# Shift of the modulation as two extra token columns, with its weights read during the projection stream

## The chip, the cores and the metric

One core of one Trainium2 chip runs the kernel. The metric is the device time of one execution in microseconds, as the median of several runs. A run's profile gives the span of the core and what each engine did: PE (TensorE, with PEld for its weight loads), DVE (VectorE), ACT (ScalarE), POOL (GpSimd) and SP (SyncE, which here only issues transfers).

## The reference

One layer of a hybrid backbone over 640 tokens: 128 context tokens and 512 latent tokens. What matters here is the modulated norm and the one input projection behind it (D_MODEL = 2048, D_IN = 7216):

```python
mod_ctx = silu(c_ctx)[None] @ w_mod + b_mod      # the same with c for the latent tokens
shift, scale, gate = jnp.split(mod, 3, axis=-1)
h = _rms_norm(x, norm_w) * (1.0 + scale[:, None]) + shift[:, None]
proj = h @ w_in
u_f, z_f, qkv, z_d, ab = jnp.split(proj, [...], axis=-1)
y_f = _fourier_mix(u_f, grid) * jax.nn.silu(z_f)
qkv = _short_conv(qkv, conv_w)
...
y_d = _rms_norm(o, gnorm_w).reshape(bsz, l, D_DELTA) * jax.nn.silu(z_d)
y = jnp.concatenate([y_f, y_d], axis=-1) @ w_out
return x + gate[:, None] * y, ...
```

All arrays are float32. There are two modulation vectors, one for all context tokens and one for all latent tokens. q, k and v (12 heads of 128) go through a short convolution and a gated-delta scan in chunks, in both directions; the context's final states are an output, and a final norm follows the layer.

## The kernel before

The kernel works on transposed activations: 16 tiles h_hi and 16 tiles h_lo of 128 rows (model channels) by 640 tokens, float32 split into a high and a low part of a faster format. A projection tile is 128 output channels. It takes, for both token halves of 320 columns (HALVES) and all 16 row tiles, three matmuls (high weight by high h, high by low, low by high), 96 in all, written by `stream` (L1272). The weights come by ACT's DMA queue in loads of half a tile into two buffers raw (`loads`, L1242), ACT makes the high part (`casts`, L1251) and POOL the low part (`lows`, L1259), five buffers each.

The **prologue** reads x, transposes and norms it (xT), and computes the modulation in pairs of row tiles (eight pairs kp). For a pair of scales, `mod_load` issues four loads of 512 KB from w_mod on SP's queue, `mod_rows` multiplies them with the two condition vectors (L421), `mod_cols` transposes and adds the parts up (L429), and `spread` writes h_hi and h_lo of the pair. While the scales arrive, the tiles k, v and q of head 0 and the gate columns ab are accumulated from h without the shift (`early_part`, L408 and L409); they are stored to ed. The shift of a pair is computed by the same steps (`shift_rows`, `shift_cols`): its columns csh are written, and `spread` computes h_hi and h_lo of the pair a second time with the shift. Pairs 0 to 2 of the shift stand between scale pairs 3 to 7, pair 3 behind them, pairs 4 to 7 among the three Fourier tiles u0 to u2, which are computed in the prologue too (`u_part`, L540). `shift_product` (L545) multiplies the shift columns with the weights of head 0 and of the gates; the result, ebias, is added to the stored early tiles later (`early_bias`, L593).

Behind the prologue the order is written out by a planner. Steps of work are generators with a rank; a step yields the engine it needs next ("P", "A", "V", "G", "S") or "poll", and is taken up when the estimate of engine times (class Estimate) says that it is due on PE's time line. The estimate starts with all engines free at the stream's first instruction. On the chip, each engine runs its instructions in the order so written and waits for semaphores. The tiles follow one another in the order of `names`: k1 q1 v1 z0 u3, then k, v, q of a head and z of the head before, and at the end k11 v11 q11 z10 f0 f1 f2 f3 z11. At a tile's end the stream waits for what it needs: k and q of head i for the scan ("delta") of head i - 2, v for the reading of the v before.

What follows a tile: `conv` evicts q, k, v from PSUM into one of two padded tiles pj (L713) and convolves; `after_z` reads PSUM for the gates z and f (L746 tanh, L749 product) and stores them; `after_u` stores u. Per head there follow `blocks`, `solve` (small triangular blocks, through two transfers over DRAM), `decay` (its last step squares q on ACT into jq and sums by a matmul, L935 and L939), `prep`, `scan` and `head_out` (L1098). `gates` (L623 to L660) comes ahead of all heads. `res_gates` (L1202, L1212) computes the residual gate in eight blocks of 256 columns behind head 0's scan. `fourier` runs for four groups in two lanes and needs u, f, the last head's solve and the residual gates. Then the output pass (L1541) multiplies y with w_out, heads 0 to 10 first, then the four Fourier groups, then head 11.

Of the kernel before, what the change touches and what calls it, by code (L numbers as in the profile page):

```python
# [9 lines left out]
F32 = mybir.dt.float32  # L10
# [7 lines left out]
P = 128  # L18
# [194 lines left out]
def hybrid_step(ctx: ExitStack, tc: tile.TileContext, x_prompt, x_sample, state_ctx, c, c_ctx,  # L213
# [53 lines left out]

    wpool = ctx.enter_context(tc.tile_pool(name="wpool", bufs=1))
# [30 lines left out]
    with tc.tile_pool(name="start", bufs=1) as st:  # L299
# [42 lines left out]

        pm0 = mbank()
# [33 lines left out]
        hi_t = [big.tile([P, NT], F32R, tag=slots[k], name="h_hi") for k in range(NK)]  # L377
        lo_t = [big.tile([P, NT], F32R, tag=slots[NK + k], name="h_lo") for k in range(NK)]


        first = (C_K, C_V, C_Q)
# [7 lines left out]
        ahead = {3: 0, 5: 1, 7: 2}  # L389
        csh = st.tile([P, NK, 32], F32, name="csh")  # L390
# [43 lines left out]
        def spread(kt, shift):  # L434
            hf = st.tile([P, NT], F32, tag="hf", name="hf", bufs=1)
            for m, a, b in ((1, 0, P), (0, P, NT)):
                x, scm = xT[:, kt, a:b], sc[:, kt, m:m + 1]
                if shift:
                    sh = csh[:, kt, m:m + 1]
                    ACT.activation(hi_t[kt][:, a:b], x, AF.Identity, bias=sh, scale=scm)  # L440
                    DVE.tensor_scalar(hf[:, a:b], x, scm, sh, ALU.mult, ALU.add)
                else:
                    ACT.mul(hi_t[kt][:, a:b], x, scm)
                    DVE.tensor_scalar(hf[:, a:b], x, scm, None, ALU.mult)
            DVE.tensor_tensor(lo_t[kt], hf, hi_t[kt], ALU.subtract)

        def scales(kp, ms):
            mo = mod_cols(pms[0], ms)
            for i in range(2):
                kt = 2 * kp + i  # L450
                DVE.tensor_scalar(sc[:, kt], mo[:, i], cols[:, 16 + kt:17 + kt],
                                  cols[:, 48 + kt:49 + kt], ALU.add, ALU.mult)
            for i in range(2):
                spread(2 * kp + i, False)

        shift_ms = {}

        def shift_rows(kp):
            shift_ms[kp] = mod_rows(pms[1], mod_load(256 * kp))

        def shift_cols(kp):
            mo = mod_cols(pms[1], shift_ms.pop(kp))
            for i in range(2):
                kt = 2 * kp + i
                DVE.tensor_scalar(csh[:, kt, 0:2], mo[:, i], cols[:, kt:kt + 1], None, ALU.add)
            for i in range(2):
                spread(2 * kp + i, True)

        def load_rest(c):
            raws = [wpool.tile([P, 8, P], F32, tag="raw", name="raw", bufs=2) for _ in range(2)]  # L470
            ACT.dma_start(out=raws[0].rearrange("p (k u) b -> p k (u b)", u=2), in_=win_v[:, 4 * c:4 * c + 4, 0:256])
            ACT.dma_start(out=raws[1][:, 0:4], in_=win_v[:, 4 * c:4 * c + 4, 256:384])
            rv = raws[0].rearrange("p (k u) b -> p u k b", u=2)
            return rv[:, 0], rv[:, 1], raws[1][:, 0:4]

        def load_first(c):
            cr = []
            for j in range(2):
                x = st.tile([P, 4, 256], F32, tag="wm", name="cr", bufs=8).rearrange("p a b -> p (a b)")[:, 0:864]
                cr.append(x.rearrange("p (k n) -> p k n", k=2))  # L480
                ks = slice(4 * c + 2 * j, 4 * c + 2 * j + 2)
                for i in range(3):
                    SP.dma_start(out=cr[j][:, :, P * i:P * (i + 1)], in_=win_v[:, ks, first[i]:first[i] + P])
                POOL.tensor_copy(cr[j][:, :, 384:432], abr[:, ks])
            return cr
# [5 lines left out]
        for kp in range(NK // 2):  # L491
# [17 lines left out]
            if kp in ahead:  # L509
                shift_rows(ahead[kp])  # L510
# [6 lines left out]
            if kp in ahead:  # L517
                shift_cols(ahead[kp])
        shift_rows(3)
        early_part(NK // 2 - 1, 0, prev)  # L520
        shift_cols(3)
        rest = load_rest(0)
        ws = [split(rest[0]), split(rest[1])]
        cr = load_first(0)
# [6 lines left out]
        ws.append(split(rest[2]))  # L531
        u_res = [[bank(), bank()], [bank(), bank()], [bank(), mbank()]]
        pc = mbank()

        def u_part(i, c, w):
            for j in range(4):
                k = 4 * c + j
                for n, (x, h) in enumerate(((w[0], hi_t), (w[0], lo_t), (w[1], hi_t))):
                    for (a, b), acc in zip(HALVES, u_res[i]):
                        PE.matmul(acc[:, 0:320], lhsT=x[:, j, :], rhs=h[k][:, a:b], start=k + n == 0,  # L540
                                  stop=k == NK - 1 and n == 2)

        def shift_product(c, cr):
            for j in range(4):
                PE.matmul(pc[32 * j:32 * j + 32, 0:432], lhsT=csh[:, 4 * c + j, :], rhs=cr[j // 2][:, j % 2, :], start=c == 0,  # L545
                          stop=c == 3, tile_position=(0, 32 * j))

        for c in range(4):
            now, ws = ws, []
            if c < 3:  # L550
                rest = load_rest(c + 1)
            steps = [[4], [5, 6], [7], []][c]
            for i in range(3):
                if i < len(steps):
                    shift_rows(steps[i])
                u_part(i, c, now[i])
                if i < len(steps):
                    shift_cols(steps[i])
                if c < 3 and i > 0:
                    ws += [split(x) for x in (rest[0:2] if i == 1 else rest[2:3])]  # L560
                if i == 0:
                    shift_product(c, cr)
                    if c < 3:
                        cr = load_first(c + 1)
# [10 lines left out]
        mc = st.tile([P, 432], F32, name="mc")  # L575
        ACT.copy(mc, pc[:, 0:432])
        for i in range(4):
            n = P if i < 3 else 48
            PE.matmul(pm[0:n, 2 * i:2 * i + 2], lhsT=mc[:, P * i:P * i + n], rhs=K("sel_mod"), start=True, stop=True)
        DVE.tensor_copy(ebias[:, 0:3].rearrange("p i m -> p (i m)"), pm[:, 0:6])  # L580
        DVE.tensor_copy(ebias[0:48, 3], pm[0:48, 6:8])
        u_res = [[x[:, 0:320] for x in r] for r in u_res]
        del pm, pms, pc
# [29 lines left out]

    def gates():
        room["th"] -= 1
        abT = g.tile([P, NT], F32, tag="th", name="abT", bufs=2)
        early_load(0, abT, 0)
        yield "A"
# [80 lines left out]
    turn = [0]  # L699

    def conv(kind, h, parts):
# [3 lines left out]
        pj = pads[turn[0] % 2]  # L705
        turn[0] += 1
        if isinstance(parts, int):
            early_load(parts, pj, 1)
            yield "A"
# [9 lines left out]
        room["pj"] += 1  # L719
        yield "A"  # L720
# [9 lines left out]
    def halves(res):  # L730
# [889 lines left out]
```

## Time and profile before

| what | us |
|---|---|
| time, median of 3 runs (lowest, highest) | 1464.56 (1462.55, 1469.27) |
| the profiled execution's own time | 1473.74 |
| its span | 1472.0 |
| first matmul of the stream | 185.9 after the span's start |
| busy time of PE, DVE, ACT, POOL | 1402.6, 705.5, 652.5, 624.5 |
| transfers | 198.59 MB |

Busy times are sums over the span; matmuls overlap in the pipeline and their ends are modelled, so a PE that is busy is not PE at its peak. Distances between the starts of matmuls say what one costs. A window's row has its limits, its length, the busy time (and number of instructions) of PE, PEld, DVE, ACT and POOL, the clock granted to PE as a share, the busy share of the 16 DMA engines and GB/s. In the timeline, a row has start, length, engine, line, operation, what it writes and reads, shape, count, and in brackets the idle time before it and what ended it; SPq and ACTq are the engines' issues of transfers.

### The profile page before, as it was taken

The page shows a single profiled execution, that of the slowest core. Times are in us where ns is not written, and L with a number is a line of the kernel's source. Part 1 is how long each engine was busy: PE and PEld are TensorE (multiplying, and loading weights), DVE is VectorE, ACT ScalarE, POOL GpSimd, SP SyncE. Part 2 cuts the span into 40 slices and gives each one's busy share as a digit, 9 for nine tenths or more (in the row PEclk, how much of TensorE's full clock was granted, in tenths as well). Part 3 has the DMA queues.
Part 4 walks back from the last instruction along what each step waited for, and adds up shares of the span by engine and source line. Part 5 has one row for each costly group of instructions (what it writes and reads, how often), then busy time and mean ns, then how long its engine had stood idle before and what let it go on. Part 6 is the DMA issues. An engine that isn't in the chain of part 4 may idle for free. (4 is left out here: it accounts for less than half of the span.)

```text
span 1472.0 us, 31131 instructions
## 1 busy us (share of the span) xinstructions
PE 1402.6 (95%) x12468; PEld 1277.2 (87%) x12468; DVE 705.5 (48%) x1474; ACT 652.5 (44%) x1694; POOL 624.5 (42%) x657
## 2 busy tenths in 40 slices
PE   6999979979899999999999999999999999999996
PEld 5676869979889898999999899989999998887885
DVE  5454445564536546462737365564747334413025
ACT  5333356444354453535454453545354333323134
POOL 2213224532534544344545354343544423337475
PEclk9999989999999999999999999999999999999999
DMA  9999543423434535352413333322324435595103
GB/s 314 292 342 293 168 129 89 116 79 104 146 108 141 150 100 151 118 158 71 106 56 101 90 85 103 89 84 68 109 66 112 135 108 179 169 303 181 43 1 143
DMA packets 251534, 198.59 MB, mean 135 GB/s; under 512 B 43449, under 2 KB 221574, under 8 KB 251262
## 3 DMA queue, kind: packets, MB, share of 16 engines
q1 hardware_dynamic: 130782, 124.77, 27.1%
q10 hardware_dynamic: 120608, 71.84, 17.0%
q8 instruction: 98, 1.61, 0.5%
q14 instruction: 46, 0.38, 0.1%
HBM read 172.57 MB, written 23.99 MB: 134 GB/s over the span
## 5 line engine op out<-in xcount | busy, mean ns | idle before, releaser
L1272 PE MATMUL mbank<-h_hi,whi 128*128 128x320 f32 x1600 | 525.5, 328 | 0.0
L1259 POOL TENSOR_TENSOR wlo<-raw,whi 128x512 fp32r<-128x512 f32 x220 | 315.2, 1438 | 443.3 <-ACT whi L1251 409.6
L1272 PE MATMUL mbank<-h_lo,whi 128*128 128x320 f32 x1600 | 497.9, 311 | 0.0
L1272 PE MATMUL mbank<-h_hi,wlo 128*128 128x320 f32 x1600 | 497.9, 311 | 0.0
L1272 PEld LDWEIGHTS mbank<-h_hi,whi 128*128 128x128 f32 x1600 | 304.8, 191 | 16.6 <-issue 11.2
L1272 PEld LDWEIGHTS mbank<-h_lo,whi 128*128 128x128 f32 x1600 | 304.9, 191 | 0.2
L1272 PEld LDWEIGHTS mbank<-h_hi,wlo 128*128 128x128 f32 x1600 | 303.9, 190 | 0.0
L1251 ACT CAST whi<-raw 128x512 fp32r<-128x512 f32 x220 | 135.8, 619 | 209.2 <-PE mbank L1272 137.4
L279 POOL TENSOR_TENSOR wlo<-raw,whi 128x512 fp32r<-128x512 f32 (+1 forms) x56 | 70.3, 1264 | 142.6 <-ACT whi L278 96.8
L1038 ACT ACTIVATE vn<-bank,s 128x128 f32<-128x128 f32 x120 | 37.5, 363 | 84.1 <-PE bank L1035 84.1
L1541 PE MATMUL mbank<-wlo,y_hi 128*128 128x512 f32 x160 | 62.7, 392 | 2.8 <-POOL wlo L279 2.0
L1541 PE MATMUL bank<-wlo,y_hi 128*128 128x512 f32 x160 | 62.7, 392 | 1.6 <-POOL wlo L279 1.6
L278 ACT CAST whi<-raw 128x512 fp32r<-128x512 f32 (+1 forms) x56 | 31.8, 587 | 71.7 <-PE bank L1541 16.7
L1541 PE MATMUL bank<-whi,y_hi 128*128 128x512 f32 x160 | 62.6, 391 | 0.7 <-ACT whi L278 0.7
L1541 PE MATMUL mbank<-whi,y_lo 128*128 128x512 f32 x160 | 62.6, 391 | 0.5 <-DVE y_lo L1428 0.5
L1541 PE MATMUL mbank<-whi,y_hi 128*128 128x512 f32 x160 | 62.9, 393 | 0.0
L1541 PE MATMUL bank<-whi,y_lo 128*128 128x512 f32 x160 | 62.7, 392 | 0.0
L837 DVE TENSOR_TENSOR tmp<-NP,XB 40x4 f32<-40x4 f32 (+6 forms) x84 | 40.0, 476 | 37.6 <-DMA NP<-pd 35.5
L924 ACT ACTIVATE E<-gb,ngg 128x128 f32<-128x128 f32 x120 | 41.2, 394 | 35.7 <-DVE AT L927 32.1
L1050 DVE SCALAR_TENSOR_TENSOR S<-S,egl,bank 128x128 f32<-128x128 f32 x72 | 21.8, 344 | 69.0 <-PE bank L1043 69.0
L1065 DVE TENSOR_TENSOR o<-o,bank 128x128 f32<-128x128 f32 x96 | 26.4, 286 | 51.4 <-ACT o L1064 35.5
L781 POOL TENSOR_TENSOR nk<-sk,cst 128x5 f32<-128x5 f32 x12 | 14.1, 1179 | 82.3 <-DVE sk L778 82.3
(329 smaller groups left out, 2568.1 us busy)
## 6 DMA issues: line engine op xcount, KB each, us to landing
raw<-in_w_in ACTq DMA_DIRECT2D x104, 512.0 KB
wm<-in_w_mod SPq DMA_DIRECT2D x64, 512.0 KB
gw<-in_w_mod SPq DMA_DIRECT2D x32, 512.0 KB
raw<-in_w_out ACTq DMA_DIRECT2D x48, 256.0 KB
gb<-gd SPq DMA_DIRECT2D x12, 640.0 KB
yd<-zs SPq DMA_DIRECT2D x16, 320.0 KB
yt<-yd SPq DMA_DIRECT2D x16, 320.0 KB
out<-res SPq DMA_DIRECT2D x10, 512.0 KB
```

What stands on the lines that cost most here:

```text
L278: ACT.copy(whi, raw_part)
L279: sub.tensor_tensor(wlo, raw_part, whi, ALU.subtract)
L781: POOL.tensor_tensor(nk, sk, K("phalf")[:, 0:5], ALU.pow)
L837: DVE.tensor_tensor(tv, NPd[:, :, i, 0:i].unsqueeze(2).broadcast_to(s4), Xd[:, :, 0:i, 0:i].rearrange("p h j c -> p h c j"), ALU.mult)
L924: ACT.activation(E[:, 1 - d], gb[:, d, P * t:P * (t + 1)], AF.Exp, bias=ngg4[:, d, h, t:t + 1])
L1038: ACT.mul(vn[:, d], pv[:, P * d:P * (d + 1)], s["s3"][:, d, tt[d]:tt[d] + 1])
L1050: DVE.scalar_tensor_tensor(Sn[:, d], S[:, d], egl4[:, d, h, tt[d]:tt[d] + 1], pu[:, P * d:P * (d + 1)], ALU.mult, ALU.add)
L1065: DVE.tensor_tensor(oo, oo, ops, ALU.add)
L1251: ACT.copy(his[c], raws[c // 2][:, 4 * (c % 2):4 * (c % 2) + 4])
L1259: POOL.tensor_tensor(lo, raws[c // 2][:, 4 * (c % 2):4 * (c % 2) + 4], his[c], ALU.subtract)
L1272: PE.matmul(pm[:, 0:320], lhsT=w, rhs=h[k][:, a:b], start=k + m == 0, stop=k == NK - 1 and m == 2)
L1541: PE.matmul(acc[t], lhsT=a[kk][:, sl], rhs=w, start=kk == order[0] and j == 0, stop=kk == order[-1] and j == 2)
```

## The change

The shift is no longer added to h. The columns of h become 642: the last two hold the shift vectors of latent and context tokens (high and low part). The second half of every tile but u has 322 columns, so that two columns of its result are the product of the shift with the weights, and these are added as a bias when the tile is evicted. The u tiles take no such columns; their product (ubias) is computed by itself and added when `fourier` reads u.

```diff
-        hi_t = [big.tile([P, NT], F32R, tag=slots[k], name="h_hi") for k in range(NK)]
+        hi_t = [big.tile([P, NT + 2], F32R, tag=slots[k], name="h_hi") for k in range(NK)]
...
+                b += 2 if hv and kind != "u" else 0
                 for k in range(NK):
+                    while b > NT and ("shift", k // 2) not in done:
+                        yield "stall"
...
-                        PE.matmul(pm[:, 0:320], lhsT=w, rhs=h[k][:, a:b], start=k + m == 0, stop=k == NK - 1 and m == 2)
+                        PE.matmul(pm[:, 0:b - a], lhsT=w, rhs=h[k][:, a:b], start=k + m == 0, stop=k == NK - 1 and m == 2)
```

In the prologue only pair 0 of the shift is left (AHEAD = 1), behind the scales; pairs 1 to 7, the product for head 0 and the u tiles move into the stream. The loads go to six slots of tiles that the heads use later, by SP's queue:

```diff
+    ring = (("AT", 2), ("AT", 2), ("gb", 1), ("gw", 1), ("KK", 2), ("KK", 2))
+    def shift_loads():
+        for n in range(4 * (NK // 2 - AHEAD) + 8):
+            while n >= sh_used[0] + len(ring):
+                yield "poll"
...
+                SP.dma_start(out=x, in_=wmv[:, 4 * j:4 * j + 4, 256 * kp:256 * kp + 256])
...
+    def shifts():
+        for kp in range(AHEAD, NK // 2):
+            while len(sh_in) < n + 4:
+                yield "poll"
+            yield "P", max(est.written(x) for x in sh_in[n:n + 4]) + 0.7
...
+            for kt in (2 * kp, 2 * kp + 1):
+                ACT.copy(hi_t[kt][:, NT:NT + 2], csh[:, kt, 0:2])
...
+            done.add(("shift", kp))
+        pc, pa = bank(), bank()
...
+        done.add("ebias")
```

`gates` and the early tiles of head 0 (`conv` with a stored tile) wait until ebias is done; the two padded tiles are handed out from a list. The evictions:

```diff
-            for a, b, ps in parts:
-                ACT.copy(pj[:, a:b], ps)
+            add = shift_of(parts)
+            for m, a, b, ps in ((1, 1, 129, parts[0][:, 0:128]), (0, 130, 322, parts[0][:, 128:320]), (0, 322, 642, parts[1][:, 0:320])):
+                ACT.activation(pj[:, a:b], ps, AF.Identity, bias=add[:, m:m + 1])
...
     def after_z(k, parts):
         yield from take("zs")
+        yield from take("pj")
+        pj = pads.pop()
+        add = shift_of(parts)
...
+            ACT.activation(pj[:, a:b], ps, AF.Identity, bias=add[:, m:m + 1])
```

with tanh and product then read from pj. `shift_u` computes ubias in two blocks as `res_gates` does, ahead of it, and `res_gates` no longer waits for head 0. The order of the tiles:

```diff
-    names = "k1 q1 v1 z0 u3".split()
-    fill = {11: "z10 f0 f1 f2 f3 z11"}
+    names = "u0 u1 u2 u3 k1 q1 v1 z0 z1 f0 f1 f2".split()
+    fill = {2: "", 11: "z10 f3 z11"}
```

Two smaller edits: `solve` reads only the 16 by 16 diagonal halves of its blocks, in eight transfers instead of four (its tile NP shrinks from 1056 to 544 columns), and `decay` places the jq matmul later:

```diff
         ACT.activation(jq, QT, AF.Square)
-        yield
+        yield "P", est.last + 1.5
```

More of the change, by code (lines that the diff above doesn't have):

```diff
@@ L437, in spread @@
                 x, scm = xT[:, kt, a:b], sc[:, kt, m:m + 1]
[L438 to L445, printed above, removed]
+                ACT.mul(hi_t[kt][:, a:b], x, scm)
+                DVE.tensor_scalar(hf[:, a:b], x, scm, None, ALU.mult)
+            DVE.tensor_tensor(lo_t[kt][:, 0:NT], hf, hi_t[kt][:, 0:NT], ALU.subtract)
         def scales(kp, ms):
@@ L453, in scales @@
             for i in range(2):
[L454 to L485, printed above, removed]
+                spread(2 * kp + i)
         def heads(kp):
@@ L530, in hybrid_step @@
             ACT.dma_start(out=ed[i], in_=ev)
[L531 to L564, printed above, removed]
+        for kp in range(AHEAD):
+            shift_in(kp, mod_cols(pms[1], shift_ms[kp]))
         rows2 = st.tile([108, P], F32, name="rows2")
@@ L574, in hybrid_step @@
         ACT.mul(nea, nea, -1.0)
[L575 to L583, printed above, removed]
+        del pm, pms
     def early_load(i, dst, at):
@@ L617, in gates @@
         early_load(0, abT, 0)
+        while "ebias" not in done:
+            yield "poll"
         yield "A"
@@ L728, in conv, with shift_of @@
         done.add((kind, h))
-    def halves(res):
-        return [(1, 129, res[0][:, 0:128]), (130, 322, res[0][:, 128:320]), (322, 642, res[1])]
+    def shift_of(res):
+        add = g.tile([P, 2], F32, tag="add", name="add", bufs=3)
+        ACT.copy(add, res[1][:, 320:322])
+        return add
     def to_tokens(src):
@@ L1128, in fourier @@
         SP.dma_start(out=uT, in_=ud[f])
+        yield "A"
+        for m, a, b in ((1, 0, P), (0, P, NT)):
+            ACT.activation(uT[:, a:b], uT[:, a:b], AF.Identity, bias=ubias[:, f, m:m + 1])
         yield "V"
@@ L1186, in fourier, with shift_u @@
         SP.dma_start(out=yd[f], in_=zs)
+        room["pj"] += 1
+        pads.append(pj)
         yield
+    def shift_u():
+        while "ebias" not in done:
+            yield "poll"
+        for i in range(2):
+            ga = yield from rows256(win_v[:, :, 256 * i:256 * i + 256], csh)
+            pg = bank()
+            for q in range(2):
+                PE.matmul(pg[:, 2 * q:2 * q + 2], lhsT=ga[:, P * q:P * (q + 1)], rhs=K("sel_mod"), start=True, stop=True)
+            DVE.tensor_copy(ubias[:, 2 * i:2 * i + 2].rearrange("p i m -> p (i m)"), pg[:, 0:4])
+            yield
+        done.add("ubias")
@@ new lines, in rows256 @@
+    def rows256(src, lhs):
+        ga = g.tile([P, 256], F32, tag="ga", name="ga", bufs=1)
+        for j in range(4):
+            gw = g.tile([P, 4, 256], F32, tag="gw", name="gw", bufs=1)
+            SP.dma_start(out=gw, in_=src[:, 4 * j:4 * j + 4])
+            yield "P", est.last + 3.0
+            pg = bank()
+            for q in range(4):
+                PE.matmul(pg[32 * q:32 * q + 32, 0:256], lhsT=lhs[:, 4 * j + q, :], rhs=gw[:, q, :], start=True, stop=True,
+                          tile_position=(0, 32 * q))
+            if j:
+                DVE.tensor_tensor(ga, ga, pg[:, 0:256], ALU.add)
+            else:
+                DVE.tensor_copy(ga, pg[:, 0:256])
+        yield
+        return ga
@@ L1190, in res_gates @@
     def res_gates():
-        while ("delta", 0) not in done:
-            yield "poll"
+        yield from shift_u()
         for i in range(8):
             ns = slice(2 * DM + 256 * i, 2 * DM + 256 * i + 256)
-            ga = g.tile([P, 256], F32, tag="ga", name="ga", bufs=1)
-            for j in range(4):
-                gw = g.tile([P, 4, 256], F32, tag="gw", name="gw", bufs=1)
-                SP.dma_start(out=gw, in_=wmv[:, 4 * j:4 * j + 4, ns])
-                yield "P", est.last + 3.0
-                pg = bank()
-                for q in range(4):
-                    PE.matmul(pg[32 * q:32 * q + 32, 0:256], lhsT=cz[:, 4 * j + q, :], rhs=gw[:, q, :], start=True, stop=True,
-                              tile_position=(0, 32 * q))
-                if j:
-                    DVE.tensor_tensor(ga, ga, pg[:, 0:256], ALU.add)
-                else:
-                    DVE.tensor_copy(ga, pg[:, 0:256])
-            bt = g.tile([2, 256], F32, tag="gbt", name="gbt", bufs=1)
+            ga = yield from rows256(wmv[:, :, ns], cz)
+            bt = g.tile([P, 4, 256], F32, tag="gw", name="gbt", bufs=1)[0:2, 0]
@@ L1289, in stream @@
             yield
-    for f in range(3):
-        after_u(f, u_res[f])
-    done = {("u", 0), ("u", 1), ("u", 2)}
+    done = {("shift", kp) for kp in range(AHEAD)}
     live = []
```

140 lines of the change are left out of this document (105 added, 35 removed).

## The prediction

> **What bounds the kernel now.** I read the page first, then the windows by stage, the waits of TensorE, and the timeline where the waits lie. The page:
>
> ```profile
> PE 1402.6 (95%) x12468; PEld 1277.2 (87%) x12468; DVE 705.5 (48%) x1474; ACT 652.5 (44%) x1694; POOL 624.5 (42%) x657
> ```
>
> TensorE (PE) carries the time, but 95% busy does not say how much can be gained. The windows by stage (length, busy time of PE, PEld, DVE, ACT, POOL, granted clock, DMA share, GB/s) do:
>
> ```profile
> 48.00:124.00 76.00, 75.29 (x643) 53.65 (x636) 37.77 (x91) 31.15 (x65) 16.51 (x16) 1.00 0.94 306
> 124.00:186.00 62.00, 59.58 (x458) 48.55 (x458) 23.16 (x40) 19.26 (x38) 18.80 (x19) 0.97 0.70 224
> 186.00:300.00 114.00, 102.58 (x956) 100.17 (x955) 59.39 (x119) 64.97 (x167) 49.54 (x59) 0.96 0.42 112
> 300.00:440.00 140.00, 127.75 (x1411) 116.11 (x1411) 69.41 (x166) 62.34 (x187) 53.27 (x65) 0.95 0.38 111
> 440.00:800.00 360.00, 359.16 (x3607) 337.76 (x3607) 194.02 (x431) 174.36 (x483) 167.17 (x176) 1.00 0.41 116
> 800.00:1150.00 350.00, 339.68 (x3600) 330.72 (x3600) 194.75 (x388) 168.24 (x468) 160.12 (x175) 0.98 0.32 89
> 1236.00:1338.00 102.00, 99.78 (x441) 81.85 (x440) 32.77 (x35) 29.95 (x54) 40.49 (x30) 1.00 0.73 240
> ```
>
> Even in the prologue's heavy part (48 to 124) PE idles only 0.7 us, although DMA is at 0.94; and 440 to 800 is full at clock 1.00. So moving work from the prologue into the stream moves PE time and saves none by itself. Loss is where PE is idle or its clock is low: 11.4 us idle and 0.04 x 114 = 4.6 us of clock in 186 to 300, 12.3 and 0.05 x 140 = 7.0 in 300 to 440, 10.3 and 0.02 x 350 = 7.0 in 800 to 1150. The waits of PE name them (us in total, times, longest):
>
> ```profile
> PE bank L939 <- ACT jq L935: 10.3, 5, 2.8
> PE bank L644 <- DVE ab L642: 9.0, 1, 9.0
> ```
>
> jq is the late wait, five times; ab is the gate chain at the stream's head; what idles in 300 to 440 comes below. How the clock follows a wait stands in the timeline of PE (start, length of a merged row, idle before in brackets):
>
> ```profile
> 205.59 0.31 PE L1272 MATMUL mbank<-h_hi,whi 128*128 128x320 f32 x1
> ...
> 209.40 0.31 PE L1272 MATMUL mbank<-h_hi,wlo 128*128 128x320 f32 x1
> ...
> 812.86 2.33 PE L939 MATMUL bank<-cst,jq 128*128 128x64 f32 x10 [2.84 <-ACT jq L935]
> ...
> 815.36 0.47 PE L1272 MATMUL mbank<-h_lo,whi 128*128 128x320 f32 x1
> 815.62 0.47 PE L1272 MATMUL mbank<-h_hi,wlo 128*128 128x320 f32 x1
> ```
>
> Between the first two rows lie 26 starts in a row, so a 320-column matmul costs 3.81 / 26 = 0.147 us at full clock, and a tile of 96 of them 14.1 us. After the wait of 2.84 us they start 0.26 us apart: nearly half clock, and the 2% of clock that 800 to 1150 lacks is this, five times.
>
> **The change part by part.** *The prologue.* These rows of PE's timeline give its border and prices:
>
> ```profile
> 124.00 0.64 PE L421 MATMUL mbank<-wm,cz 128*32 128x256 f32 x8 [0.71 <-DVE ev L529]
> ...
> 160.47 1.93 PE L421 MATMUL mbank<-wm,cz 128*32 128x256 f32 x32
> ...
> 177.89 0.93 PE L545 MATMUL mbank<-cr,csh 128*32 128x432 f32 x8
> ...
> 185.92 0.39 PE L1272 MATMUL mbank<-h_hi,whi 128*128 128x320 f32 x1
> ```
>
> The first row waits for ev, so the early tiles end at 124; the stream starts at 185.9. The 62 us between hold the three u tiles (3 x 14.1 = 42.2), the shift product (4 x 0.93, with switching 4.1), and four shift pairs at 1.93 plus about 0.5 for transposes and switching (9.6): 56 us of work. The other 6 us are waits for weights, half clock and switching, and they go. Three more shift pairs lie before 124 and leave it, so the new prologue ends near 124 - 3 x 2.8 = 116; I call that E. The second pass of h (10 instructions on ACT and DVE per pair) goes off engines that have room there, and is costed at nothing.
>
> *Seven shift pairs in the stream.* Each brings 4 loads on SP, 32 matmul instructions, an ACT copy, two transposes and a few small DVE and ACT steps: 7 x 2.4 = 17 us of PE, as before. Its loads:
>
> ```profile
> wm<-in_w_mod SPq DMA_DIRECT2D x64, 512.0 KB
> ```
>
> 28 loads are 14.7 MB, the product's 8 loads 3.5 MB (2 x 432 columns each), and u0 to u3 and k1 take 5.2 MB by ACT's queue (2048 x 128 x 4 bytes each): 23.4 MB. At the 306 GB/s of 48 to 124 that is 77 us; at the 224 of 124 to 186 it is 105. PE's own work there is 5 x 14.1 + 17 + 5 = 92 us. The loads can't start before the prologue's memory is free, after the ev stores: about E + 5. So all pairs and the bias come at E + 82 to E + 110, between PE running out or not. The planner's clock starts with empty engines, so it should place the first pair's matmuls some 5 us too early. New wait: 0 to 20 us; I take 12 (5 late start, 3 half clock, 4 rate), nearer to the 306 because that stage too had both queues full. Behind it on PE stands everything; on ACT a late bias holds up the casts behind the bias step, and those feed PE again. On SP the u stores and the first heads' loads are queued among the ring's waits; nobody needs them before the bias.
>
> *The gates* now wait for the bias, in the middle of the stream, where the planner knows the engines' state. The 16 us of 186 to 300 (11.4 and 4.6) go; a similar wait on the same chain costs 0 to 14, I take 5.
>
> *The tile order.* Before, four tiles stand between k1 and k2, and PE comes to wait for head 0's scan:
>
> ```profile
> 303.75 0.31 PE L1272 MATMUL mbank<-h_hi,wlo 128*128 128x320 f32 x1
> ...
> 325.66 1.30 PE L1098 MATMUL bank<-cst,o 128*128 128x128 f32 x5 [3.62 <-DVE o L1087]
> ...
> 327.90 0.63 PE L1272 MATMUL mbank<-h_hi,whi 128*128 128x320 f32 x1
> ```
>
> For 24 us no tile's matmul runs; PE waits between the links of one head's chain. The chain takes 140 us from the gates at the stream's head (185.9) to its end (325.7). A head costs PE about 23 us beside its tiles: stream of 186 to 1234, less 50 tiles (705), losses (50) and residual gates (21), by 12. Afterwards k2 ends after 13 tiles (183), 22 of shifts, 5 of shift_u, 5 of residual gates, 3 of gates and some 40 of two heads: E + 258. Head 0 is done at E + 92 (the bias, 10 us behind the lower bound) + 140 = E + 232. So that wait goes: 12.3 + 7.0 = 19 us, of which I leave 3 to come back.
>
> *jq.* The planner now places the matmul 1.5 us later. The five waits were 2.1 us in the mean and 2.8 at most, so 0.6 and up to 1.3 us each remain; 10.3 + 7.0 = 17 us go and 5 come back. The Trainium skill ("TensorE: Matmul & The Clock Gate", part 1, the HAM clock gate) has the clock halved after an idle window of about 3.4 us; by that rule waits under 3 us would cost no clock, this item would be 10 and the time 1447. The row above, half clock after 2.84 us, decides against it.
>
> *Added on PE.* 49 tiles x 48 matmuls x 2 columns at 0.147/320 us: 2.2 us. shift_u is two blocks like the residual gates' eight:
>
> ```profile
> L1202 PE MATMUL bank<-gw,cz 128*32 128x256 f32 x256 | 20.9, 399 | 0.3 <-ACT KK L796 0.3
> ```
>
> 20.9 / 8 = 2.6 each, 5.2 for two; the product in two banks, 0.6 more. Together 8 us.
>
> *Beside PE.* Each of 16 z and f tiles gets three evictions with bias and one small copy. What ACT waits for:
>
> ```profile
> ACT whi L1251 <- PE mbank L1272: 137.4, 99, 7.0
> ```
>
> Three evictions at up to 0.44 us (the row of z10 below, 320 columns) and a copy of two columns make about 1.5 us x 16 = 24 us on ACT, 46% instead of 44%. The casts wait 137 us for PE and not PE for them, so their five buffers cover it; without that cover it is up to 24 us, below nothing it can't go. solve's 8 loads for 4 put up to 2 us into a chain that the order gives tens of us. Fourier's two bias steps are about 1 us of ACT each time.
>
> **Sum.** Gone: 6 + 16 + 19 + 17 = 58. Added: 8. New waits: 12 + 5 + 3 + 5 = 25. Net -25 us: the profiled 1473.74 (span 1472.0 and 1.7 around it) becomes 1449. That execution was 9 us above the median 1464.56; the same difference on the median gives **1440 us**.
>
> **The rivals.** *Everything fits.* The plan overlaps, and of the 25 us of new waits 5 stay: -45, 1420. For it: 440 to 800 shows a plan without idle time. Against: the plan's start was wrong before too (ab, 9 us).
>
> *The waits come back elsewhere.* Gates and first heads lose as before, 35 instead of the 8 that I left them: +2, 1467. For it: the same chain of 140 us, now 80 us later. Against: seven tiles more stand ahead of k2.
>
> *The tail is exposed.* Only z10, f3 and z11 follow q11, three tiles fewer.
>
> ```profile
> 1127.37 0.44 ACT L746 ACTIVATE zs<-mbank 128x320 f32<-128x320 f32 x1 [0.37 <-PE mbank L1272]
> ...
> 1132.97 1.97 SPq L864 DMA_DIRECT2D DD<-xd  x4
> ...
> 1156.58 0.44 SPq L1128 DMA_DIRECT2D uT<-ud  x1
> ...
> 1184.52 0.32 SPq L1186 DMA_DIRECT2D yd<-pj  x1
> ```
>
> z10's last eviction is at 1127.4, so its tile began and q11 ended near 1112; call it T. A Fourier group takes 28 us (1156.6 to 1184.5) and can start after solve, which reads its last transfer at 1133 to 1135 and has some 9 us to go: T + 32. The stream ends at T + 77 (42 of tiles and the 35 us of other work of 1112 to 1232), and eleven heads of the output pass hide 11 x 15 x 102/441 = 38 us more: T + 115. In two lanes all four groups are done near T + 92; one behind the other they take until T + 144, while the pass has 10 us in the first three: 19 us of wait and 5 of half clock and of y's way to PE. That gives -1, 1464. Against it: the lanes use separate buffers.
>
> *DMA starves the stream (slower).* Of 224 GB/s the tiles take 1.05 MB per 14.1 us, 74; 150 remain for the shifts: 18.2 MB last 121 us. PE has work to E + 80 for the pairs that come at E + 106, and waits some 10 us more for the bias: 36 of wait and 6 of half clock in place of the 12, +5. At 140 GB/s it is 9 us more: +14, 1479. It decides against the change below some 147. For it: a ring of six slots that PE must free. Against: the 224 is a mean over a stretch in which loading had ended early, with share 0.70.
>
> *The biases aren't late but the waits stay for another reason* (jq slower under the fuller ACT, nothing recovered at the start) would be 1465; I give it little.
>
> **How the numbers follow.** Forecast 0.50, everything fits 0.24, waits come back 0.09, tail 0.06, starved 0.08, last one 0.03. A measurement of this kernel can tell about 0.5%, 7.3 us, from no change. The first two are faster: 0.74; the starved case is slower: 0.08; the rest is the same: 0.18. The range goes from the good case to the exposed tail, 1419 to 1464: out of it stay the starved case, half of the returned waits and a little below, under 0.2.
>
> **What would show it.** Right: ev ends near 116; waits for jq under 5 us in total; no stretch of 20 us without L1272 between 250 and 450 (its new line number); PEclk 0.98 or more from 186 to 440; gaps of a few us at the first pair's matmuls. Wrong: a long wait of k1's second half for h_lo columns or of ACT for the bias; waits of the output pass for y of the Fourier groups; ACT casts late for PE. If the span falls by over 50 us, there was loss that I don't see in busy time; if by under 8, one of the three returns.

## The result, and the profile after

The changed kernel takes 1484.61 us (median of 4 runs, 1483.22 to 1485.51), the kernel before, run beside it, 1464.64 (1462.55 to 1469.27): a ratio of 1.0131, interval 1.0105 to 1.0157. It is slower by 20 us where 25 us faster were forecast. The profiled execution took 1485.51 us (span 1483.7), 0.9 us above its median; that of before had been 9 us above its own. Between the two profiled executions lie therefore only 12 us, and what is read from their traces has to add up to that, not to the 20 us of the medians.

From the page after, the busy times:

```profile
PE 1410.5 (95%) x12572; PEld 1285.2 (87%) x12572; DVE 686.6 (46%) x1452; ACT 670.7 (45%) x1784; POOL 618.4 (42%) x649
```

The windows by stage (columns as before; the stream now starts at 110):

```profile
48.00:110.00 62.00, 62.00 (x540) 51.71 (x540) 23.86 (x55) 20.82 (x47) 17.25 (x14) 0.99 0.81 246
110.00:190.00 80.00, 74.44 (x603) 64.67 (x605) 12.46 (x39) 17.54 (x47) 22.12 (x26) 0.94 0.93 289
190.00:300.00 110.00, 96.44 (x718) 86.96 (x711) 49.87 (x103) 56.75 (x145) 35.58 (x33) 0.94 0.52 144
300.00:440.00 140.00, 137.55 (x1486) 126.01 (x1487) 57.77 (x144) 59.55 (x174) 54.57 (x66) 0.98 0.43 126
440.00:800.00 360.00, 349.48 (x3734) 327.11 (x3734) 200.42 (x426) 178.86 (x500) 158.90 (x174) 0.99 0.39 111
800.00:1170.00 370.00, 363.71 (x3593) 356.58 (x3592) 206.86 (x429) 196.81 (x555) 171.93 (x186) 1.00 0.31 84
1170.00:1240.00 70.00, 64.46 (x686) 60.92 (x686) 35.21 (x108) 33.72 (x92) 24.79 (x29) 0.98 0.46 142
1248.00:1350.00 102.00, 101.03 (x445) 82.02 (x446) 30.61 (x42) 31.98 (x60) 39.35 (x31) 1.00 0.71 239
```

Read idle time (length less busy PE) and clock (what the clock lacks times the length) together; idle time at half clock counts in both, some 3 us at most in one row. The shift stage, 110 to 190, loses 5.6 + 4.8 = 10.4 us. The gates, 190 to 300, lose 13.6 + 6.6 = 20, where 16 were lost before. The first heads, 300 to 440, lose 2.4 + 2.8 = 5 instead of 19. From 440 to 1240 it is 10.5 + 3.6, 6.3 and 5.5 + 1.4, together 27; before, 440 to 1150 lost 18. The stage from 440 to 800, which was full, is no longer full. The waits of PE name what came:

```profile
PE bank L900 <- DVE DD L889: 15.3, 6, 6.1
PE bank L651 <- DVE ab L649: 6.2, 1, 6.2
PE bank L569 <- DMA sx<-in_w_mod: 5.5, 3, 4.6
PE bank L630 <- ACT abT L518: 3.2, 1, 3.2
```

No wait for jq is left in the list. In its place stands DD: the first matmuls of the block inverses (`solve`, L900) wait for VectorE's transpose of blocks that come back over DRAM (L889). Before, that wait was 2.8 us in all:

```profile
PE bank L879 <- DVE DD L868: 2.8, 3, 1.2
```

The list of after has one more of this kind under another name: `PE bank L900 <- DVE ubias L1226`, 2.7 us, is head 0's block inverses near 300, and the copy to ubias that ended the wait stood on VectorE right behind the transpose of DD, for whose loads VectorE had idled 5 us. The timeline of PE at the longest one (idle before in brackets):

```profile
778.42 1.29 PE L900 MATMUL bank<-DD,g 32*32 32x32 f32 x80 [6.15 <-DVE DD L889]
779.64 0.64 PE L1319 MATMUL mbank<-h_hi,whi 128*128 128x320 f32 x1
...
781.14 0.47 PE L1319 MATMUL mbank<-h_hi,wlo 128*128 128x320 f32 x1
781.41 0.47 PE L1319 MATMUL mbank<-h_hi,whi 128*128 128x320 f32 x1
```

Behind the wait the stream's matmuls start 0.27 us apart, the half clock that the prediction had read behind jq.

### The profile page after: what moved, and what is told of

It is laid out like the page before. It is cut to its first block, busy times and chain, and to the rows that moved or that the text cites. A ratio compares the mean times of both kernels' runs of the same rounds, so it can differ in the third digit from the quotient of the medians.

```text
span 1483.7 us, 31493 instructions
## 1 busy us (share of the span) xinstructions
PE 1410.5 (95%) x12572; PEld 1285.2 (87%) x12572; DVE 686.6 (46%) x1452; ACT 670.7 (45%) x1784; POOL 618.4 (42%) x649
## 5 line engine op out<-in xcount | busy, mean ns | idle before, releaser
L1319 PE MATMUL mbank<-h_hi,whi 128*128 128x320 f32 (+1 forms) x1696 | 558.7, 329 | 0.0
L1303 POOL TENSOR_TENSOR wlo<-raw,whi 128x512 fp32r<-128x512 f32 x232 | 327.7, 1416 | 527.1 <-ACT whi L1295 410.1
L1319 PE MATMUL mbank<-h_lo,whi 128*128 128x320 f32 (+1 forms) x1696 | 529.0, 312 | 0.0
L1319 PE MATMUL mbank<-h_hi,wlo 128*128 128x320 f32 (+1 forms) x1696 | 528.7, 312 | 0.0
L1319 PEld LDWEIGHTS mbank<-h_hi,whi 128*128 128x128 f32 x1696 | 323.4, 191 | 25.0 <-issue 21.3
L1319 PEld LDWEIGHTS mbank<-h_lo,whi 128*128 128x128 f32 x1696 | 323.7, 191 | 0.0
L1319 PEld LDWEIGHTS mbank<-h_hi,wlo 128*128 128x128 f32 x1696 | 322.8, 190 | 0.2 <-POOL wlo L1303 0.2
L283 POOL TENSOR_TENSOR wlo<-raw,whi 128x512 fp32r<-128x512 f32 (+1 forms) x44 | 55.2, 1263 | 86.9 <-ACT whi L282 66.8
L1049 POOL TENSOR_SCALAR kd<-k,edl 128x128 f32<-128x128 f32 x96 | 40.6, 436 | 15.5 <-PE bank L1064 15.2
L933 POOL TENSOR_TENSOR gb<-gb,cst 128x640 f32<-128x640 f32 x24 | 34.8, 1456 | 22.9 <-DMA gb<-gd 20.5
```

Source lines behind the costliest of these rows:

```text
L283: sub.tensor_tensor(wlo, raw_part, whi, ALU.subtract)
L933: POOL.tensor_tensor(gv, gv, masks[d].unsqueeze(1).broadcast_to([P, 5, P]), ALU.add)
L1049: POOL.tensor_scalar(kd[:, d], k[:, tt[d], :], edl4[:, d, h, tt[d]:tt[d] + 1], 1.0, ALU.mult, ALU.mult)
L1303: POOL.tensor_tensor(lo, raws[c // 2][:, 4 * (c % 2):4 * (c % 2) + 4], his[c], ALU.subtract)
L1319: PE.matmul(pm[:, 0:b - a], lhsT=w, rhs=h[k][:, a:b], start=k + m == 0, stop=k == NK - 1 and m == 2)
```

## The experiments

Every run is timed beside the kernel before on the same chip, and its ratio is to that kernel; 0.1% is 1.5 us. Four theories stood. **1**: matmuls run slower because the change moved the tiles' addresses (1b: because h rows became longer). **2**: the wait for jq went on to the next link of its head, and it and the gates' waits are places in the planner's order that are some us too early, so that a later due time removes them; the rival is that they go on to a further link each time. **3**, formed after the first eight runs: most of the cost is one such place, the block inverses', and the guard on jq (the due time 1.5 us later) made it worse. **4**, formed last: the later due times are worth as much without the change.

### The pace of the matmuls

A window of the output pass without idle time, in the kernel before and in the changed one:

```profile
1350.00:1430.00 80.00, 80.00 (x355) 66.24 (x354) 15.59 (x21) 24.23 (x49) 52.05 (x40) 1.00 0.10 33
```

```profile
1350.00:1430.00 80.00, 80.00 (x347) 64.80 (x346) 18.06 (x22) 22.94 (x48) 50.70 (x38) 1.00 0.13 44
```

At clock 1.00, 355 matmuls of 512 columns fit before and 347 after, some 225 and 231 ns each; over the whole pass the starts of neighbours lie 226.8 and 231.8 ns apart. Nothing in the diff touches this pass. A 32-byte tile (ubias) had moved all large tiles by 32 bytes, so I tried that first.

```diff
     ubias = const.tile([P, 4, 2], F32, name="ubias")
+    const.tile([P, 8], F32, name="gap")
```

> The changed kernel with one unused 32-byte column of constants behind the shift bias, so that every large tile behind it (weights, raw weights, even h tiles) starts at a multiple of 64 bytes again, as in the kernel before; odd h tiles (rows 8 bytes longer) stay at 32. Theory 1 (addresses set the matmul pace): output pass matmuls of 512 columns at 227 to 230 ns apart instead of 232, stream matmuls at 147 instead of 148, and 3 to 10 us off, 1475 to 1482 us. Rival (the pace is the run's or the chip's, or comes from the longer h rows themselves): 232 ns and 1484 us as the changed kernel.

It took 1.0139 (1.0112 to 1.0165): no gain, and the starts in the output pass still lay 232 ns apart. With the h_hi tiles aligned too (`NT + 16` columns):

> The same, and the h_hi tiles 656 columns wide so that all of them start at multiples of 64 bytes; odd h_lo tiles stay at 32. Theory 1: 227 ns in the output pass and the whole 8 to 10 us off, 1474 to 1477 us. If the odd h tiles do not matter it equals the run with the unused column alone. Rival: 1484 us.

1.0143 (1.0108 to 1.0178), and 230 to 232 ns. The same line in the kernel before:

> The kernel before with the unused 32-byte column alone, nothing else changed: all large tiles start 32 bytes off a multiple of 64. Theory 1: output pass matmuls 232 ns apart instead of 227, stream matmuls 148, 8 to 10 us slower than the kernel before, 1473 to 1475 us. Rival: 227 ns and 1464 to 1465 us.

1.0002 (0.9982 to 1.0023), and 227 ns. Theory 1 falls: 32 bytes change nothing when all tiles move together. What also changed is the distance of the h tiles, 2592 bytes for 2560.

```diff
-        hi_t = [big.tile([P, NT], F32R, tag=slots[k], name="h_hi") for k in range(NK)]
+        hi_t = [big.tile([P, 642], F32R, tag=slots[k], name="h_hi")[:, 0:NT] for k in range(NK)]
...
```

(the same for h_lo; three small tiles share others to make room)

> The kernel before with h rows allocated 8 bytes longer (642 columns, of which 640 are used, so that tile k starts at k times 2592 bytes instead of 2560); to make room, three small scratch tiles share others. No column is added to any matmul. Theory 1b (the pace comes from the longer rows: the moving and the stationary tile no longer start at the same address modulo 256 bytes): output pass matmuls of 512 columns 232 ns apart instead of 227, stream matmuls of 320 columns 147 instead of 146.4, and 8 to 11 us slower than the kernel before, 1473 to 1477 us. Rival (the pace comes from the two extra columns, or from what else runs in the changed kernel): 227 ns and the time of the kernel before, 1464 to 1467 us.

The same window in that run:

```profile
1350.00:1430.00 80.00, 80.00 (x347) 64.70 (x346) 14.40 (x19) 23.30 (x48) 51.23 (x39) 1.00 0.08 27
```

347 again: the longer rows alone set the pace, with no column in any matmul. The stream's 320-column matmuls start 146.9 ns apart instead of 146.4. The time is 1.0014 (0.9986 to 1.0041), 2 us more with 6 as the bound, less than the 8 to 11 I expected of it; by the paces it would be 7, and why so little of it shows is open. The last kernel of this group holds matmuls alone:

> Matmuls alone, none of the reference computed: the loop of the output pass (stationary rows of 128 columns, moving weights of 512) with rows at the same address modulo 256 bytes as the weights (group da), shifted by 32 to 224 bytes (db to dh), and with tiles 2592, 2624, 2688 and 2816 bytes apart (sb, sc, sd, se); then the loop of the stream with 320 columns at 2560 and 2592 bytes (ha, hb) and with 322 columns at 2592 and 2816 (hc, hd). Theory 1b: da, se, ha at 227, 227 and 146.5 ns from one matmul to the next, sb at 231 to 233, hb at 147 to 148, hd faster than hc, and part of db to dh slow as sb. Rival (other engines' reads and writes make the difference, not the addresses alone): all of the output loop at 227 within 1 ns.

The groups of PE (busy us, mean ns of one behind the bar):

```profile
L234 PE MATMUL dd<-wt,rows 128*128 128x512 f32 x144 | 33.9, 396 | 0.0
L234 PE MATMUL sb<-wt,rows 128*128 128x512 f32 x144 | 33.6, 394 | 0.0
L234 PE MATMUL dg<-wt,rows 128*128 128x512 f32 x144 | 33.1, 391 | 0.0
L234 PE MATMUL da<-wt,rows 128*128 128x512 f32 x144 | 32.8, 389 | 0.0
L234 PE MATMUL se<-wt,rows 128*128 128x512 f32 x144 | 32.8, 389 | 0.0
```

From start to start it is 226.7 ns in da and se, 231.7 to 232.1 in sb, sc and sd, 229.0 in dg and 232.3 to 234.2 in the other shifts. So no other engine is needed for it: the pace is full when the stationary and the moving tile start at the same address modulo 256 bytes. Rows of 2560 bytes, as in the kernel before, keep that relation from tile to tile; the addresses in the two whole kernels were not read. The stream's loop hardly shows the effect: 146.6 ns in ha and 146.7 in hb (in the kernel it was 146.4 and 146.9), 147.9 and 148.3 in hc and hd. Going by the step from 320 to 512 columns, two columns should cost 0.8 ns; they cost 1.2 at 2592 bytes and 1.7 at 2816, so theory 1b, which had hd faster than hc, is shown for the 512-column matmuls only.

### The waits of the later heads

The smallest part of the change undone, the due time of the squared-q matmuls:

```diff
         ACT.activation(jq, QT, AF.Square)
-        yield "P", est.last + 1.5
+        yield
```

> The changed kernel with the squared-q matmuls guarded as before (the due time is the default again, not 1.5 us behind the last planned ScalarE work). Theory 2 (the wait only moved to the next link of each head, the block inverses' matmuls): waits before the squared-q matmuls return (about 10 us with half clock behind them), waits before the block-inverse matmuls after VectorE's transpose fall from 27 us to under 6, and the time stays within 5 us of the changed kernel. Rival (the guard does what it says, the other waits have another cause): 10 to 17 us slower than the changed kernel, 1494 to 1501 us.

1.0087 (1.0061 to 1.0114), some 6 us faster than the change. Its waits:

```profile
PE bank L900 <- DVE DD L889: 7.6, 6, 2.6
PE bank L960 <- ACT jq L956: 0.2, 1, 0.2
```

The jq waits do not return, which theory 2 had expected, and the DD waits fall to half. (The 27 us that the expectation gives to DD are the whole loss of 440 to 1240; its own waits are the 15.3 of the list, and 18.2 to 21.5 in a_again, a_pad and a_padhi.) So the guard had nothing to cover here, and without it the other wait is shorter. The issues of two transfers of one head show how; first the changed kernel, then this run (last numbers: first and last start):

```profile
L929 SPq DMA_DIRECT2D gb<-gd x1: 381/381/381, 768.6 to 768.6; - x1
...
L885 SPq DMA_DIRECT2D DD<-xd x4: 308/550/1017, 770.7 to 773.0; - x4
L889 DVE STREAM_TRANSPOSE DD<-DD x1: 512/512/512, 777.9 to 777.9; 128x320 f32<-128x320 f32 x1
```

```profile
L929 SPq DMA_DIRECT2D gb<-gd x1: 381/381/381, 760.1 to 760.1; - x1
...
L885 SPq DMA_DIRECT2D DD<-xd x4: 307/406/418, 782.8 to 784.2; - x4
L889 DVE STREAM_TRANSPOSE DD<-DD x1: 511/511/511, 787.5 to 787.5; 128x320 f32<-128x320 f32 x1
```

With the guard a head's decay ends later in the order, and the next head's 640 KB of gb are issued 2 us ahead of the DD loads instead of 23: the transpose then starts 7.2 us behind the first DD issue instead of 4.7. Both waits of about 6 us in the changed kernel (6.15 and 5.48) stand behind such a pair; two more pairs stand ahead of a wait of 1 us and of none. Over all heads from 440 on the ranges meet: 5.3 to 7.3 us with the pair (in one of the four VectorE was busy until then), 3.3 to 5.2 in the other heads of the changed kernel, 3.4 to 6.0 in the run without the guard. No run moved the gb load alone, so its part is read from the traces and not isolated. Now the place in the plan:

```diff
         DVE.transpose(DD[:, 2:4].rearrange(f2), DD[:, 0:2].rearrange(f2))
-        yield
+        yield "P", est.last + 6.0
```

> The changed kernel with the block inverses' matmuls due 6 us later in the planner's order, one line of each head. Theory 2: the waits for VectorE's transpose (27 us in all, two of them 6 us) fall under 6 us and 8 to 15 us come off, 1470 to 1477 us. Rival (as the squared-q wait did, the wait goes on to the next link of the head's chain: the matmuls behind the transposes, the block corrections, the scan): the waits named there grow by as much and the time stays within 5 us, 1480 to 1488 us.

0.9990 (0.9969 to 1.0012): 20 us off by one line, more than I expected, and level with the kernel before. The waits of 440 to 1240 hold no DD any more, nor does head 0 wait for ubias, and the next links took little (S had 2.3 us without the line):

```profile
PE bank L909 <- ACT M L902: 4.8, 4, 1.7
PE bank L1037 <- DVE S L1071: 3.9, 4, 2.1
```

The rival, that the wait goes on along the chain, falls. To see whether this was cover or the luck of a new order, other due times and the change once more:

> The changed kernel with the block inverses' matmuls due 3 us later instead of 6. Theory 3 (what comes off is the wait that the later due time covers): the waits of about 1 us go, the two of 6 us fall to about 3, so 8 to 14 us off the changed kernel, 1.003 to 1.008 of the kernel before. Rival (any edit of the plan reshuffles the order, and 6 us was a lucky draw): anything, also no gain (1.010 or more).

> The same with 9 us. Theory 3: no wait before these matmuls is left, as with 6 us, and 0.997 to 1.002 of the kernel before; the head's chain ends 3 us later, which nothing in the middle heads waits for. Rival (a lucky draw): anything from 0.99 to 1.013.

> The changed kernel itself once more, on the same chip as the two others: 1.011 to 1.016 of the kernel before by its first timing.

The change itself again 1.0131 (1.0104 to 1.0157). With 3 us 1.0082 (1.0056 to 1.0109), with 9 us 1.0058 (1.0040 to 1.0076). The windows of the later heads and of the handover to the output pass, with 3, 6 and 9 us:

```profile
440.00:1170.00 730.00, 716.49 (x7345) 689.26 (x7344) 405.86 (x849) 378.33 (x1063) 339.42 (x362) 0.99 0.36 99
1170.00:1260.00 90.00, 83.46 (x762) 74.77 (x762) 39.61 (x140) 40.60 (x101) 24.91 (x30) 0.96 0.44 141
```

```profile
440.00:1170.00 730.00, 718.53 (x7458) 688.80 (x7459) 413.77 (x865) 380.16 (x1069) 338.51 (x362) 1.00 0.36 100
1170.00:1260.00 90.00, 88.37 (x706) 78.06 (x707) 44.66 (x137) 43.00 (x104) 28.59 (x34) 1.00 0.50 163
```

```profile
440.00:1170.00 730.00, 721.42 (x7553) 692.24 (x7551) 413.17 (x860) 381.23 (x1072) 343.52 (x363) 1.00 0.36 100
1170.00:1260.00 90.00, 82.75 (x608) 72.54 (x595) 38.84 (x131) 39.22 (x96) 26.34 (x32) 0.98 0.46 150
```

Both times lie outside what theory 3 gave, the second one clearly. In the heads the answer is graded: the DD waits are 15.3 us without the line, then 4.9, 0 and 0, and PE idles 16.8 us (10.5 + 6.3 above), then 13.5, 11.5 and 8.6. With the clock of the rows it is 20, 21, 11 and 9, so in this one profile 3 us had no gain there yet. The handover is not graded: it idles 6.5, 1.6 and 7.3 us, because with 3 and 9 us the output pass comes to wait for y, in both runs:

```profile
PE mbank L1587 <- ACT y_hi L1472: 5.4, 2, 4.1
```

With the clock of these rows the handover costs 10.1, 1.6 and 9.1 us; in the changed kernel without the line its loss was one of the two long DD waits. So both hold: what comes off in the heads is cover, and 7 to 9 us more hang on how the end of the order happens to fall. With both lines (6 us, and the default for jq):

> The changed kernel with the block inverses' matmuls due 6 us later, and the squared-q matmuls due by the default again: both guards together. Theory 3 (the block inverses' early place in the plan is the cost, and the guard on squared q made it worse by sliding two large loads together): with the block inverses covered the squared-q guard is worth under 4 us either way, 1462 to 1470 us. Rival (the squared-q guard is needed once the other wait is gone): waits of about 10 us before the squared-q matmuls, 1472 us or more.

1.0036 (1.0014 to 1.0058): without the guard 7 us slower. The time (1473.76 us) is on the rival's side, but the trace shows no jq wait; it shows the same 5.4 us for y at the handover. The rival's mechanism isn't there, and theory 3's "under 4 us" missed.

### The gates

```diff
-            yield "P", max(est.written(x) for x in sh_in[n:n + 4]) + 0.7
+            yield "P", max(est.written(x) for x in sh_in[n:n + 4]) + (5.5 if kp == AHEAD else 0.7)
...
         early_bias(0, abT, 0)
-        yield
+        yield "P", est.last + 3.5
...
+        yield "P", est.last + 6.5
         pb = bank()
```

> The changed kernel with three matmul groups due later in the planner's order: the first rows of the moved shift 4.8 us later, the gates' projections 3.5 us and the gates' running sums 6.5 us later, so that stream matmuls stand where TensorE waited. Theory 2 (these waits are a plan that is too early, nothing that must be waited for): the waits of 4.6, 3.2 and 6.2 us fall under 1.5 us together, the clock between 110 and 300 us rises from 0.94 to 0.97 or more, 10 to 18 us off, 1467 to 1475 us. Rival (the waits move to the heads behind, which start later): under 5 us off, 1480 us or more.

1.0089 (1.0054 to 1.0125), 6 us off, with an interval that overlaps that of the change; theory 2 had given 10 to 18. The wait for ab goes and the one for abT falls from 3.2 to 1.5, but the window shows how little comes of it alone:

```profile
190.00:300.00 110.00, 102.30 (x883) 92.83 (x881) 52.98 (x108) 60.07 (x154) 38.45 (x36) 0.95 0.55 151
```

7.7 us idle instead of 13.6, and hardly more clock. The DD waits (15.9 us) stay as they were.

### The same lines without the change, and all together

> The kernel before with the block inverses' matmuls due 6 us later, nothing else. Theory 3: it waited only 2.8 us there, so within 4 us of the kernel before, 1461 to 1469 us. Rival (the line is a gain of its own, whatever the change does): 8 us or more faster, under 1458 us.

0.9974 (0.9953 to 0.9995): 4 us, as theory 3 gave.

> The kernel before with the guard on the squared-q matmuls alone (due 1.5 us later), the smallest part of the change. Theory 3: the five waits of 10.3 us there go, waits before the block inverses' matmuls take their place (over 8 us), time within 5 us of the kernel before, 1460 to 1470 us. Rival (the prediction's step): waits under 5 us and half of its clock loss gone, 10 to 14 us faster, 1451 to 1456 us.

0.9967 (0.9944 to 0.9989), 5 us, between the two theories. Against the profile of before, half of the jq waits stay and some DD wait comes:

```profile
PE bank L879 <- DVE DD L868: 6.0, 4, 2.3
PE bank L939 <- ACT jq L935: 5.4, 6, 1.6
```

But the profile of before was of an execution 9 us above the median. The run with the 32-byte tile alone (b_shift) is the kernel before in all that matters here, its time is the same, and its profiled execution, at 1462.75 us, waits as the run with the guard does:

```profile
PE bank L880 <- DVE DD L869: 6.2, 6, 1.5
PE bank L940 <- ACT jq L936: 5.2, 5, 2.5
```

With the longer rows (b_h642) it is 6.1 for jq and 5.6 for DD. So no trace shows that the guard alone covers a wait in the kernel before, and where its 5 us come from is open.

> The kernel before with both guards (squared q 1.5 us, block inverses 6 us later). Theory 3: neither wait is left and the 10 to 17 us that the prediction counted come off, 1448 to 1457 us. Rival (the waits go on to a third link): within 5 us of the kernel before.

0.9938 (0.9917 to 0.9958): 9 us off, just under the 10 to 17 that theory 3 gave; of jq 0.3 us of waiting is left and of DD none. Then all later due times (`solve`, shift rows, gates) in the changed kernel, and those that exist in the kernel before:

> The changed kernel with all later due times at once: block inverses 6 us, first moved shift rows 4.8 us, gates' projections 3.5 us, gates' running sums 6.5 us later. Theory 3 (each wait was a place in the plan, and they are independent): the 18 to 20 us of the block inverses' line and the 5 us of the gates' lines add, 0.994 to 0.997 of the kernel before. Rival (they share the same later waits): as with the block inverses' line alone, 0.998 to 1.000.

> The kernel before with the same lines (block inverses, gates' projections, gates' running sums) and the guard on squared q. Theory 4 (the later due times are worth something in either kernel, and what is left of the change itself, columns, longer rows and the moved stage, is worth nothing or less): 0.988 to 0.993 of the kernel before, below the changed kernel with the same lines. Rival (the change itself gains once the plan is repaired): not below the changed kernel with the same lines.

0.9926 (0.9900 to 0.9952) and 0.9950 (0.9927 to 0.9973). With its order repaired the change is 11 us faster than the kernel before and 30 us faster than the change as it was; its advantage over the kernel before with the same lines, 0.24%, lies within the intervals. The later heads and the gates' stage of the changed kernel so repaired:

```profile
440.00:1170.00 730.00, 721.07 (x7587) 692.33 (x7586) 410.17 (x855) 383.83 (x1079) 342.23 (x372) 1.00 0.36 102
...
190.00:300.00 110.00, 101.89 (x766) 92.50 (x757) 52.68 (x106) 61.27 (x158) 38.54 (x35) 0.98 0.57 156
```

The repairs add up (30 us for 20 + 6 alone), as theory 3 has it, if not more; theory 4 fell, since the kernel before gains 7 us from lines that give the changed one 30. Last, the change with the block inverses due 6 us later and without its columns; this kernel leaves out the streamed tiles' own shift:

> The changed kernel with the block inverses' matmuls due 6 us later, without the two columns: h rows of 640 columns as in the kernel before, matmuls of 320 columns in both halves; it leaves out the streamed tiles' own shift (the eviction adds the first bias column of constants instead), all loads, rows and casts of the moved shift stay. Theory 1b (columns and longer rows cost what their matmuls show, 2.2 us plus 9 us of pace): output pass back at 227 ns, 9 to 13 us faster than with them, 0.990 to 0.993 of the kernel before. Rival (hidden elsewhere): within 5 us, 0.996 or more.

1.0109 (1.0070 to 1.0149): 17 us slower than with the columns, not faster. The output pass is back at 355 matmuls in the same 80 us, so the pace came back as expected. But the planner counts with 320 columns and writes another order, and this order waits elsewhere: at the handover, 1170 to 1260, PE idles 9.7 us where the run with the columns (a_dd) idles 1.6, from 300 to 440 6.0 where that idles 2.1, and it waits for S 7.0 us, 3.9 there. In this kernel an edit's price can't be read from a time alone when the edit also changes the order.

## Why the prediction was wrong

Measured by the profiled executions, the prediction's steps against what the runs showed:

- *The prologue* (E = 116): the stream starts at 110.2. Right in kind, and 6 us better; what gave them is not separated.
- *Shift stage* (12 us): 10.4. Right, and for the reason given: the planner's clock starts empty, and the first pair's matmuls stand 4.6 us early. DMA ran at 289 GB/s, so the stream was not starved.
- *Tile order* (19 us of the first heads go, 3 come back): 5 are left. Right.
- *The gates* ("the planner knows the engines' state"; 16 go, 5 come back): 20 are lost. This step failed. The chain from the bias to ab stands 3 and 6 us too early again, in the middle of the stream as at its head: 9.4 of the 13.6 us idle in this stage are abT and ab, 2.7 are head 0's block inverses and 1.4 the loads of the product. Due later, the two waits fall from 9.4 to 1.5 us, and with everything repaired 110 to 300 runs at clock 0.98 instead of 0.94.
- *jq* (17 go, 5 come back): this step failed, and most of the miss hangs on it. The jq waits went, with the guard and without it, but 27 us are lost from 440 to 1240. I priced the waits that the list named, and did not ask which instruction would be late next in the same head; the list of before already had it (2.8 us for DD). One due time took 20 us off, the part of it at the handover with some luck. And the 17 us themselves were the loss of one execution, 9 us above its median: "nearly half clock, five times" is four times there (in windows of 50 us from 800 to 1150, clock 0.93 once and 0.97 three times), and the kernel with the 32-byte tile loses from 800 to 1150 only this:

```profile
800.00:1150.00 350.00, 342.81 (x3677) 333.80 (x3677) 196.16 (x393) 171.61 (x474) 162.42 (x180) 1.00 0.34 94
```

That is 7 us idle, with clock 0.97 in one of the windows of 50 us, where the prediction had 10.3 + 7.0; with the longer rows (b_h642) it is 8 us idle at 1.00. The forecast then carried the 9 us over to the changed kernel as a fixed difference between profile and median; there it was 0.9.

- *Added on PE* (8 us): the terms counted were right (shift_u 5.6 for 5.2), but rows of 2592 bytes slowed the matmuls on y and on h, which were put at nothing. The output pass takes 218 us, 2.3% of it is 5; in the stream, 2736 matmuls of 320 columns start 147.1 ns apart instead of 146.4, and 2352 of 322 at 148.5 where 147.2 were due: 1.9 + 3.1. The 3.1 belong to the two columns rather than to the rows, since the matmuls alone cost 148.3 with aligned rows too. About 10 us by count; the run with the longer rows alone shows 2 us in its time, with 6 as its bound.

Sum of the misses: 15 for the gates, 22 for the later heads, 2 to 10 for the pace, less 6 for the prologue, make 33 to 41. The profiled executions are what these numbers come from, and there 36.5 are to be explained (1449 forecast, 1485.5 measured); the 45 between the medians hold 8 more, the difference of 9 that was carried over. On the rivals: the wait did come back elsewhere, but in the later heads and the gates and not with the first heads; the tail and the starved stream did not happen.

What the prediction said of the clock gate stands: in these traces half clock follows waits of 2.8 as well as 6.2 us. By the Trainium skill ("TensorE: Matmul & The Clock Gate", part 1, the HAM clock gate) the clock is halved after an idle window of about 3.4 us. Here half clock does not follow every short wait either: four of the five jq waits of before were followed by it, and one of the five in the run with the 32-byte tile, the one of 2.5 us.

## What to carry to other kernels

The wait that the list names need not be the one that counts once the order is a new one: before counting its price as a gain, list the chain's other links with their slack, and look which transfers move together once a step ends later. Where an order is planned, test a change together with the due times it needs, and read each stage's idle time beside the total, since a new order moves the time by 7 to 9 us of its own here. Read a wait's price from more than one execution, or from one near the median: here one trace showed twice the loss of another. A tile that gets a few columns longer changes the start addresses of all tiles behind it; round its length so that the addresses of the matmul's two operands keep their relation. Here that was worth 2 us, at most 6.

## What the runs showed of the hardware

- The pace of a 512-column matmul depends on where its two operands start: 226.7 ns when stationary and moving tile agree modulo 256 bytes, 229.0 with the stationary tile 192 bytes on, 232 to 234 with the other multiples of 32. Tiles 2816 bytes apart keep it, 2592, 2624 and 2688 lose it (231.7 to 232.1). Why is open; aligning the tiles to 64 bytes did not bring it back (231 to 232 ns in a_pad and a_padhi).
- Where a load of 640 KB was issued 2 us ahead of four of 40 KB on the same queue, the transpose of what they brought stood 5.3 to 7.3 us behind their first issue, in the other heads 3.3 to 5.2. This is read from four heads of one trace and not isolated.
- Half clock can follow a wait of TensorE of 1.5 to 2.8 us, and need not: it followed four of five jq waits in the execution of before, one of five in that of b_shift.
